# Scores of the second layer issued one span of keys at a time, two small softmax operations folded into others, and the last norm stored by halves

## The chip, the cores and the metric

The kernel runs on one core of a Trainium2 chip. The metric is the device time of one execution in microseconds; an engine is named as the profile names it (PE is TensorE, DVE VectorE, ACT ScalarE, POOL GpSimd, SP SyncE). The change is compared with the kernel before by the median of several runs.

## The reference, cut to what matters

A trunk of two layers over 1024 tokens of width 1024, all in float32. Layer 0 mixes tokens by dilated windows and is not touched. Layer 1 is causal differential attention with 8 heads; each head has two attention maps over the same values, and the second is subtracted from the first.

```python
s = jnp.einsum('bqhcd,bkhcd->bchqk', qblk, k).astype(jnp.float32) * scale   # c: the two maps
s = jnp.where(kpos[None, :] <= qpos[:, None], s, -jnp.inf)
p = jax.nn.softmax(s, axis=-1)
a = p[:, 0] - lam * p[:, 1]
o = jnp.einsum('bhqk,bkhd->bqhd', a, v)
...
o = rmsnorm(o, subln) * (1.0 - lambda_init)
y = o.reshape(B, S, DIFF_WIDTH) * jax.nn.silu(gate)
h = h + rmsnorm(y @ w_out, norm_post[i])
```

## The kernel before

Float32 products are made of two halves: each operand is split into a high and a low part, and a product is three matmuls (`wh` with `XH`, `wh` with `XL`, `wl` with `XH`; the low by the low is dropped). A matmul is 128 x 128 by up to 512 columns. A PSUM tag (`pj` for projections, `s` for scores, `pt` for transposes, `u` for outputs) has two banks that take turns.

TensorE's order is the program's own (`manual_schedule`); the order on the other engines and of the DMAs is set by the compiler's scheduler from its own estimate. On TensorE layer 1 mixes two streams. The first is a list of *steps*, each with a due time in units of heads, sorted by it. The second is a *filler*, a generator of the projections of later heads (`pqk`), values (`pv`), gates (`pg`) and, at the end, the first part of the output product (`pe`). After each step, `fill.at` runs filler until as much of it is spent as belongs to that step's due time:

```python
for _, (due, step) in steps:
    step()
    fill.at(max(due, 0) / end * len(heads))
```

So a step itself stands in the queue right behind the filler of the step before it.

The steps of a head are these. `load(part)` fetches one map's queries (`qh`, `ql`) and keys (`ka`) through SyncE; there are two buffers for each tag, so the load for a head waits until the scores of the same map in the head before have been read. `scores(i, s)` is for block i of 128 queries (0 to 7) and map s: the block has (i + 1) x 128 keys, in one span for blocks 0 to 3 and in two spans for blocks 4 to 7, each of which takes one `s` bank. TensorE writes a span (`sc`, two matmuls); VectorE adds the mask and takes the row's minimum on the way into the tile `pm` (`CUSTOM_DVE_ANT_0`, L954; scores are negated, so the minimum is the largest), with a short read of the accumulated value behind it. With two spans the two minima are joined (L957); for map 0 a constant of 10 ln 2 is taken off (L960), which makes the stored probabilities 2^10 times as large. Then ScalarE takes the exponential of the whole row with its sum (L961). For map 1, VectorE makes the factor (L970, L971) and subtracts the map from map 0 (L973); `pm0` of the block is then final. `pm1` has a single buffer.

`transposes(c, k2)` turns four 128 x 128 squares of the blocks 2c and 2c+1 on TensorE (`tp`, L984), and splits them into `ph` (ScalarE, L989) and `pl` (VectorE, `low` at L122). `product(c, k2)` multiplies them by the values (`ob`, L1004). `norm` and `gate` finish half a head; `gate` ends with two stores of `y_d` through SyncE.

At the end `out_rest` runs the output product for 8 blocks of 128 tokens (`po`, L391), and `post_norm` on each: two sums out of PSUM (`pn`, L492), squares on ScalarE, `pss` and `v` on VectorE, the power -1/2 on GpSimd (`r`), then `pn` times `r` times g (L496) and the sum with the residual `hb` (L497), stored as one DMA of 512 KB.

## Time and profile before

| | |
|---|---|
| median of 3 runs | 1971.28 us (1967.11 to 1976.27) |
| profiled execution | 1973.98 us, its span 1972.1 us |
| TensorE busy | 1888.0 us, 96% of the span |
| VectorE busy | 985.4 us, 50% |
| ScalarE busy | 885.3 us, 45% |
| GpSimd busy | 784.2 us, 40% |
| mean granted TensorE clock | 0.986 |

A row of instructions gives line, engine, operation, what is written and what is read, shape and count; behind the bar the busy time in us and the mean ns of one; behind the next bar the time for which its engine stood idle just before, and what ended it. A row in order of time begins with its start and its length in us and ends, in brackets, with the idle time before it. A row of waits gives who waited for whom: us in total, times, longest. Layer 1's heads run from about 1430 to 1880 us.

### The profile page before, as it was taken

Reading aid. Unit: us, or ns where it says so; the run is one execution under the profiler, and the core shown is the slowest. Engines: PE = TensorE matmul, PEld = TensorE weight load, DVE = VectorE, ACT = ScalarE, POOL = GpSimd, SP = SyncE. Lnnn points to the kernel's source line nnn. Section 1 sums busy time; section 2 is a strip of 40 time slices with the busy share of each in tenths; the row PEclk is TensorE's granted clock in tenths of the full one; section 3 lists DMA queues with packets and bytes.
Section 4 is the critical chain, followed back from the end, with each engine's and each line's share of the span. In section 5 each row is a group of like instructions: output and inputs, shape, how many; then the busy total and the mean of one; then the engine's idle time right before and its main releaser. Section 6 shows DMA issues by size and latency. Waiting matters only on the chain.

```text
span 1972.1 us, 29075 instructions
## 1 busy us (share of the span) xinstructions
PE 1888.0 (96%) x10008; PEld 1587.9 (81%) x10008; DVE 985.4 (50%) x2618; ACT 885.3 (45%) x2043; POOL 784.2 (40%) x553
## 2 busy tenths in 40 slices
PE   7999999999999999999999878999989899999897
PEld 5788888888888888888888767788878798897786
DVE  5311221135555555555555635550177877778626
ACT  4212112135656565656565555342244455446532
POOL 0000001154585867676776532320742435423011
PEclk9999999999999999999999979999999999999899
DMA  6424344277798989898989798442644565556643
GB/s 225 161 91 133 117 145 155 91 233 219 213 294 239 296 242 283 249 280 259 271 267 267 237 329 217 165 167 87 207 155 132 181 213 182 166 182 196 239 158 128
DMA packets 217539, 397.90 MB, mean 202 GB/s; under 512 B 40880, under 2 KB 123312, under 8 KB 217392
## 3 DMA queue, kind: packets, MB, share of 16 engines
q1 hardware_dynamic: 217392, 396.04, 63.8%
q8 instruction: 80, 1.31, 0.3%
q14 instruction: 67, 0.55, 0.1%
HBM read 254.87 MB, written 132.71 MB: 197 GB/s over the span
## 4 chain that ended last, share of the span: by engine, by line
PE 74%; DMA 10%; DVE 7%; POOL 3%; ACT 3%; issue 2%; SPq 1%; POOLq 0%; ACTq 0%; DVEq 0%
PE pqk L276 29%; PE pv L213 17%; PE pg L276 8%; PE po L391 4%; PE sc L603 3%; PE sc L951 3%; PE pe L444 2%; PE tp L626 2%; PE up L653 2%; PE ob L1004 2%; DMA ql<-qk_d 2%; DMA raw<-in_dil_w_out_dram 1%; DMA qk_d<-r 1%; PE tp L984 1%; DMA wb<-wt_d 1%
## 5 line engine op out<-in xcount | busy, mean ns | idle before, releaser
L276 PE MATMUL pqk<-XL,wh 128*128 128x512 f32 x1024 | 418.7, 409 | 0.0
L276 PE MATMUL pqk<-XH,wh 128*128 128x512 f32 x1024 | 408.3, 399 | 1.7 <-DVE t L252 1.7
L276 PE MATMUL pqk<-XH,wl 128*128 128x512 f32 x1024 | 408.6, 399 | 0.0
L122 POOL TENSOR_TENSOR wl<-raw,wh 128x1024 fp32r<-128x1024 f32 x59 | 141.7, 2401 | 512.3 <-ACT wh L184 509.7
L613 ACT ACTIVATE pm<-pm,st 128x128 f32<-128x128 f32 (+1 forms) x384 | 170.4, 444 | 149.5 <-DVE st L610 148.6
L276 PEld LDWEIGHTS pqk<-XH,wh 128*128 128x128 f32 x1024 | 193.2, 189 | 31.5 <-DVE t L252 3.5
L276 PEld LDWEIGHTS pqk<-XH,wl 128*128 128x128 f32 x1024 | 193.5, 189 | 26.9
L276 PEld LDWEIGHTS pqk<-XL,wh 128*128 128x128 f32 x1024 | 193.1, 189 | 26.9
L122 DVE TENSOR_TENSOR pp<-tp,pp 128x512 fp32r<-128x512 f32 (+2 forms) x192 | 104.3, 543 | 132.5 <-ACT pp L630 131.7
L184 ACT CAST wh<-raw 128x1024 fp32r<-128x1024 f32 x96 | 100.6, 1047 | 144.4 <-PE pqk L276 65.8
L961 ACT ACTIVATE pm<-pm,mx 128x256 f32<-128x256 f32 (+7 forms) x128 | 99.4, 777 | 126.8 <-DVE mx L960 61.1
L213 PE MATMUL pv<-vwh,XH 128*128 128x512 f32 x384 | 153.0, 398 | 2.0 <-ACT XH L158 2.0
L213 PE MATMUL pv<-vwh,XL 128*128 128x512 f32 x384 | 153.0, 398 | 2.0 <-DVE XL L122 1.3
L213 PE MATMUL pv<-vwl,XH 128*128 128x512 f32 x384 | 152.2, 396 | 0.0
L122 DVE TENSOR_TENSOR vs<-pv,vs 128x512 fp32r<-128x512 f32 x64 | 44.2, 690 | 202.2 <-ACT vs L518 194.7
L610 DVE CUSTOM_DVE_ANT_0 pm<-sc,masks 128x128 f32<-128x128 f32 (+1 forms) x384 | 119.1, 345 | 27.2 <-PE sc L603 26.5
L630 ACT CAST pp<-tp 128x512 fp32r<-128x512 f32 (+2 forms) x192 | 89.6, 467 | 80.7 <-PE up L653 62.2
L954 DVE CUSTOM_DVE_ANT_0 pm<-sc,md 128x512 f32<-128x512 f32 (+3 forms) x192 | 102.6, 551 | 38.0 <-PE sc L951 35.5
L122 DVE TENSOR_TENSOR wl<-raw,wh 128x1024 fp32r<-128x1024 f32 x37 | 49.1, 1326 | 137.0 <-ACT wh L184 136.7
L251 POOL TENSOR_TENSOR r<-t 128x512 f32<-128x512 f32 x64 | 84.4, 1319 | 80.2 <-DVE t L250 79.1
L518 ACT CAST vs<-pv 128x512 fp32r<-128x512 f32 x48 | 28.1, 586 | 186.8 <-PE pv L213 186.8
L276 PE MATMUL pg<-XH,wh 128*128 128x512 f32 x256 | 103.1, 403 | 5.0 <-DVE t L252 5.0
(514 smaller groups left out, 4435.4 us busy)
## 6 DMA issues: line engine op xcount, KB each, us to landing
qk_d<-rh SPq DMA_DIRECT2D x64, 512.0 KB
qk_d<-r SPq DMA_DIRECT2D x64, 512.0 KB
qh<-qk_d SPq DMA_DIRECT2D x128, 256.0 KB
ql<-qk_d SPq DMA_DIRECT2D x128, 256.0 KB
ka<-qk_d SPq DMA_DIRECT2D x64, 512.0 KB
v_d<-vs SPq DMA_DIRECT2D x48, 512.0 KB
raw<-in_dil_qk_dram SPq DMA_DIRECT2D x48, 512.0 KB
vt<-v_d SPq DMA_DIRECT2D x48, 512.0 KB
```

The source lines that it names most:

```text
L122: return eng.tensor_tensor(o, full, hi.bitcast(F32), ALU.subtract)
L184: nc.scalar.copy(wh, raw)
L213: nc.tensor.matmul(o, lhsT=l, rhs=r_, start=first and k == 0, stop=last and k == 3 * KT - 1, skip_group_check=True)
L251: nc.gpsimd.tensor_sub(put(r[0]), nat(t1), nat(t2))
L276: nc.tensor.matmul(o, lhsT=l[:, kt, :], rhs=r_[:, kt, tok], start=kt == 0 and k == 0, stop=kt == KT - 1 and k == 2)
L391: nc.tensor.matmul(banks[c], lhsT=l[:, kt, ts(n)], rhs=r_[:, ts(c, 512)], start=first and k == 0, stop=last and k == 2,)
L603: nc.tensor.matmul(sc[:, cols], lhsT=q[:, ts(b)], rhs=kv, start=k == 0, stop=k == 1)
L610: nc.vector.tensor_tensor_reduce(pm[:, cols], sc[:, cols], m[:, m.shape[1] - w_ :], 1.0, 3.0e38, ALU.add, ALU.min, st[:, 0, j : j + 1])
L613: nc.scalar.activation(pm[:, cols], pm[:, cols], AF.Exp, bias=st[:, 0, j : j + 1], scale=-1.0, accum_out=st[:, 1, j : j + 1])
L630: nc.scalar.copy(pp[:, 0, :w_], tp[:, :w_])
L954: nc.vector.tensor_tensor_reduce(pm[:, k0:k1], sc[:, :w_], m_, 1.0, 3.0e38, ALU.add, ALU.min, mx[:, j : j + 1])
L961: nc.scalar.activation(pm[:, :wq], pm[:, :wq], AF.Exp, bias=mx[:, 0:1], scale=-1.0, accum_out=den)
```

## The change

Three things. First, `scores` takes one span at a time. A block with two spans has two steps for each map, whose due times are a quarter and three quarters of the way through the map's share, instead of one at its half.

Second, the two small operations go. The second span's reduction starts from the first span's minimum instead of a constant, so that its own result is the minimum of both; and the factor 2^10 is no longer put in by way of the exponent but taken care of where the transposes are split (`ph` and `pl` are scaled by `DEN_SHIFT` = 2^-10), with the constants of the norm adjusted.

Third, in the last norm VectorE multiplies by g without waiting for `r`, and then does each half of the row in one instruction with its own store.

```diff
+            @staticmethod
+            def spans(i):
+                wq = (i + 1) * P
+                cut = wq - max(256, wq - 512) if wq > 512 else 0
+                return [(0, cut), (cut, wq)] if cut else [(0, wq)]
...
-            def scores(self, i, s):
+            def scores(self, i, s, j):
...
-                for j, (k0, k1) in enumerate(spans):
...
-                    nc.vector.tensor_tensor_reduce(
-                        pm[:, k0:k1], sc[:, :w_], m_, 1.0, 3.0e38, ALU.add, ALU.min, mx[:, j : j + 1])
-                if cut:
-                    nc.vector.tensor_tensor(mx[:, 0:1], mx[:, 0:1], mx[:, 1:2], ALU.min)
-                if s == 0:
-                    nc.vector.tensor_scalar_add(mx[:, 0:1], mx[:, 0:1], -10 * math.log(2.0))
+                k0, k1 = self.spans(i)[j]
...
+                nc.vector.tensor_tensor_reduce(
+                    pm[:, k0:k1], sc[:, :w_], m_, 1.0, mx[:, 0:1] if j else 3.0e38,
+                    ALU.add, ALU.min, mx[:, j : j + 1])
+                if k1 < wq:
+                    return
                 nc.scalar.activation(
-                    pm[:, :wq], pm[:, :wq], AF.Exp, bias=mx[:, 0:1], scale=-1.0, accum_out=den)
+                    pm[:, :wq], pm[:, :wq], AF.Exp, bias=mx[:, j : j + 1], scale=-1.0, accum_out=den)
...
-                nc.scalar.copy(ph[:, :w_], tp[:, :w_])
-                low(nc.vector, pl[:, :w_], tp[:, :w_], ph[:, :w_])
+                nc.scalar.mul(ph[:, :w_], tp[:, :w_], DEN_SHIFT)
+                nc.vector.scalar_tensor_tensor(
+                    pl[:, :w_], tp[:, :w_], DEN_SHIFT, ph[:, :w_].bitcast(F32), ALU.mult, ALU.subtract)
...
             for i in range(NB):
+                n = len(hd.spans(i))
                 for s in range(2):
-                    due = h + SPAN * (i * (i + 1) + (s + 0.5) * (i + 1)) / 72
-                    steps.append((due, lambda hd=hd, i=i, s=s: hd.scores(i, s)))
+                    for j in range(n):
+                        due = h + SPAN * (i * (i + 1) + (s + (j + 0.5) / n) * (i + 1)) / 72
+                        steps.append((due, lambda hd=hd, i=i, s=s, j=j: hd.scores(i, s, j)))
...
-        nc.vector.scalar_tensor_tensor(t, t, r, g_b, ALU.mult, ALU.mult)
-        eng.tensor_add(res, t, res)
-        return res
+        if eng is nc.vector:
+            nc.vector.tensor_mul(t, t, g_b)
+            for c in range(2):
+                cols = ts(c, 512)
+                nc.vector.scalar_tensor_tensor(
+                    res[:, cols], t[:, cols], r, res[:, cols], ALU.mult, ALU.add)
+                yield cols, res
...
-            nc.sync.dma_start(out_v[n], o)
+            for cols, o in post_norm(op, n, p0, p1, cos, hb, nc.vector):
+                nc.sync.dma_start(out_v[n][:, cols], o[:, cols])
```

What it makes of the order, at three places. Up to layer 1 the order is the same. The first place is TensorE's queue in head 1 at block 4. `sc` are scores (two matmuls to a span), `pqk` projections of a later head. Before, the two spans of map 0 and, five projections on, those of map 1:

```order
L951 MATMUL sc_14200<-ka_13904,qh_13902 128x384
L951 MATMUL sc_14200<-ka_13904,ql_13903 128x384
L951 MATMUL sc_14204<-ka_13904,qh_13902 128x256
L951 MATMUL sc_14204<-ka_13904,ql_13903 128x256
L276 MATMUL pqk_14161<-XH_78,wh_14147 128x512
L276 MATMUL pqk_14161<-XL_79,wh_14147 128x512
L276 MATMUL pqk_14161<-XH_78,wl_14148 128x512
L276 MATMUL pqk_14161<-XH_78,wh_14147 128x512
L276 MATMUL pqk_14161<-XL_79,wh_14147 128x512
L951 MATMUL sc_14218<-ka_13918,qh_13916 128x384
L951 MATMUL sc_14218<-ka_13918,ql_13917 128x384
```

Now, at the same place:

```order
L967 MATMUL sc_14180<-ka_13888,qh_13886 128x384
L967 MATMUL sc_14180<-ka_13888,ql_13887 128x384
L277 MATMUL pqk_14141<-XH_78,wh_14127 128x512
L277 MATMUL pqk_14141<-XL_79,wh_14127 128x512
L277 MATMUL pqk_14141<-XH_78,wl_14128 128x512
L277 MATMUL pqk_14141<-XH_78,wh_14127 128x512
L967 MATMUL sc_14188<-ka_13888,qh_13886 128x256
L967 MATMUL sc_14188<-ka_13888,ql_13887 128x256
L277 MATMUL pqk_14141<-XL_79,wh_14127 128x512
L277 MATMUL pqk_14141<-XH_78,wl_14128 128x512
L277 MATMUL pqk_14141<-XH_78,wh_14127 128x512
L967 MATMUL sc_14198<-ka_13902,qh_13900 128x384
```

Four of the projections moved between the two spans, and three stand ahead of map 1.

The second place is the end of the same head on TensorE: block 7, map 1. Before, both spans stand together, and behind them come 20 projections, 6 products, 3 transposes and 4 small sums (`sm`) until the first transpose that reads blocks 6 and 7 (`tp_14614`):

```order
L951 MATMUL sc_14494<-ka_13918,qh_13916 128x512
L951 MATMUL sc_14494<-ka_13918,ql_13917 128x512
L951 MATMUL sc_14498<-ka_13918,qh_13916 128x512
L951 MATMUL sc_14498<-ka_13918,ql_13917 128x512
L276 MATMUL pqk_14447<-XH_78,wl_14154 128x512
```

Now ten projections, the 6 products and the 3 transposes stand between the first span (`sc_14463`) and the last (`sc_14492`), and this is all that is left ahead of that transpose:

```order
L967 MATMUL sc_14492<-ka_13902,ql_13901 128x512
L277 MATMUL pqk_14411<-XH_78,wh_14133 128x512
L277 MATMUL pqk_14411<-XL_79,wh_14133 128x512
L277 MATMUL pqk_14411<-XH_78,wl_14134 128x512
L1044 MATMUL sm_14524<-ones_12631,sq_14421 128x1 x4
L277 MATMUL pqk_14574<-XH_78,wh_14560 128x512
L277 MATMUL pqk_14574<-XL_79,wh_14560 128x512
L277 MATMUL pqk_14574<-XH_78,wl_14561 128x512
L277 MATMUL pqk_14574<-XH_78,wh_14560 128x512
L277 MATMUL pqk_14574<-XL_79,wh_14560 128x512
L277 MATMUL pqk_14574<-XH_78,wl_14561 128x512
L999 MATMUL tp_14582<-ident_80,pm0_14297 128x128
```

The transpose kept its place, and the last span moved towards it (one more projection, the tenth, stands right ahead of the transpose and is left out here). On SyncE the loads that follow these scores, for map 1 of head 2, stood so before, with the stores of `y_d` among them:

```order
L268 DMA qh_14548<-qk_d_67 64x1024 x2
L268 DMA ql_14549<-qk_d_67 64x1024
L384 DMA y_d1_64<-sq_14283 128x512
L384 DMA y_d1_64<-os__14282 128x512
L268 DMA ql_14549<-qk_d_67 64x1024
L270 DMA ka_14550<-qk_d_67 128x1024
```

and stand so now, behind the stores and the load of a gate:

```order
L1066 DMA sil_in_14661<-sil_d1_66 128x512
L385 DMA y_d1_64<-sq_14261 128x512
L385 DMA y_d1_64<-os__14260 128x512
L269 DMA qh_14516<-qk_d_67 64x1024 x2
L269 DMA ql_14517<-qk_d_67 64x1024 x2
L271 DMA ka_14518<-qk_d_67 128x1024
```

The third place is VectorE's queue at the very end, the last block's norm. Before:

```order
L492 TENSOR_TENSOR pn_19016<-po_18986,XH_78 128x512
L497 TENSOR_TENSOR hb_18968<-pn_18972,hb_18968 128x1024
L492 TENSOR_TENSOR pn_19016<-po_18987,XL_79 128x512
L494 TENSOR_TENSOR pss_19015<-s2_19014 128x1
L134 TENSOR_SCALAR v_19023<-pss_19015 128x1
L496 SCALAR_TENSOR_TENSOR pn_19016<-pn_19016,r_19024,cos_2235 128x1024
L497 TENSOR_TENSOR hb_19012<-pn_19016,hb_19012 128x1024
```

and now (`cos` holds g here):

```order
L493 TENSOR_TENSOR pn_18902<-po_18872,XH_78 128x512
L502 SCALAR_TENSOR_TENSOR hb_18852<-pn_18856,r_18864,hb_18852 128x512 x2
L493 TENSOR_TENSOR pn_18902<-po_18873,XL_79 128x512
L495 TENSOR_TENSOR pss_18901<-s2_18900 128x1
L499 TENSOR_TENSOR pn_18902<-pn_18902,cos_2235 128x1024
L135 TENSOR_SCALAR v_18909<-pss_18901 128x1
L502 SCALAR_TENSOR_TENSOR hb_18898<-pn_18902,r_18910,hb_18898 128x512 x2
```

The product with g stands between `pss` and `v`, and the pairs of halves take the places of the two instructions of the full row.

## The prediction

> **What bounds the kernel now.** I read the page first, then one window over the stage that the change touches (layer 1's heads, from the first score to the last transposes), then TensorE's waits, and last the order of time around single waits.

> ```profile
> span 1972.1 us, 29075 instructions
> PE 1888.0 (96%) x10008; PEld 1587.9 (81%) x10008; DVE 985.4 (50%) x2618; ACT 885.3 (45%) x2043; POOL 784.2 (40%) x553
> PE 74%; DMA 10%; DVE 7%; POOL 3%; ACT 3%; issue 2%; SPq 1%; POOLq 0%; ACTq 0%; DVEq 0%
> 1430.00:1880.00 450.00, 418.44 (x2571) 367.89 (x2569) 341.33 (x937) 235.98 (x464) 164.11 (x112) 0.98 0.57 183
> ```

> TensorE is the bound, and its instructions are the same before and after. Its queue runs in program order, so the change can only move the time by what TensorE waits, by its clock, and by what lies behind its last matmul. The last row is the stage (columns as on the page: PE, PEld, DVE, ACT, POOL busy, clock, DMA share): 450 us, TensorE idle for 31.6, VectorE busy for 341.3, 76%, the fullest engine beside it. TensorE's waits of the whole run:

> ```profile
> PE sc L951 <- DVE mx L954: 17.9, 16, 2.5
> PE sc L951 <- DMA ka<-qk_d: 7.8, 2, 6.7
> PE pv L213 <- DVE vs L122: 2.9, 1, 2.9
> PE tp L984 <- DVE pm L973: 2.6, 4, 0.9
> ```

> All four lie in this stage. The first is what the change is about: a score needs one of two PSUM banks, and VectorE has not yet reduced what stands in it. By the width of the span that waits (idle time behind the bar):

> ```profile
> L951 PE MATMUL sc<-ka,qh 128*128 128x512 f32 x80 | 34.4, 430 | 6.2 <-DVE mx L954 6.1
> L951 PE MATMUL sc<-ka,qh 128*128 128x384 f32 x48 | 17.8, 370 | 4.2 <-DVE mx L954 4.2
> L951 PE MATMUL sc<-ka,qh 128*128 128x256 f32 x48 | 15.3, 318 | 7.8 <-DVE mx L954 7.6
> ```

> It is no steady lack of VectorE time (76%), but a queue that is late at moments. One of them, block 4 of head 0:

> ```profile
> 1441.20 1.61 DVE L973 SCALAR_TENSOR_TENSOR pm<-pm,mx,pm 128x384 f32<-128x384 f32 x1
> 1442.73 1.22 DVE L1030 TENSOR_TENSOR nd<-den 128x4 f32<-128x4 f32 x1
> 1443.88 0.68 DVE L954 CUSTOM_DVE_ANT_0 pm<-sc,md 128x512 f32<-128x512 f32 x1
> 1444.62 0.39 PE L951 MATMUL sc<-ka,qh 128*128 128x256 f32 x1 [1.75 <-DVE mx L954]
> ```

> **Part 1, the small operations.** The rows that price them (busy, mean ns):

> ```profile
> L957 DVE TENSOR_TENSOR mx<-mx 128x1 f32<-128x1 f32 x64 | 22.8, 357 | 0.7
> L960 DVE TENSOR_SCALAR mx<-mx 128x1 f32<-128x1 f32 x64 | 9.5, 148 | 0.7
> L122 DVE TENSOR_TENSOR pl<-tp,ph 128x512 fp32r<-128x512 f32 x45 | 30.8, 684 | 1.7 <-ACT ph L989 1.6
> L1047 DVE SCALAR_TENSOR_TENSOR os__15635<-os__15635,subln,rt 128x512 f32<-128x512 f32 x1 | 0.7, 748 | 0.0
> L957 DVE TENSOR_TENSOR mx<-mx x64: 147/154/2250, 1446.0 to 1877.7; 128x1 f32<-128x1 f32 x64
> ```

> The minimum of two spans (L957) and the shift by a factor of 2^-10 (L960) go: 22.8 + 9.5 = 32.3 us of VectorE. The low half `pl` turns from a two-operand into a scaled three-operand instruction; the nearest row that reads PSUM, a tile and a scalar (L1047) takes 748 against 684, so 80 of them add at most 80 x 0.064 = 5.1. The second span's reduction now starts from a column instead of a constant; no row shows that form, and I bound it by nothing and by the same 0.064 each, 64 x 0.064 = 4.1, and take 2. The scaled copy `ph` on ScalarE (236 of 450 us busy) is hidden by the slack of that engine; without it, it would lengthen the step from a transposition to its product, which the program sets 0.2 of a head apart, some 11 us of 56. So VectorE gives up 32.3 - 5.1 - 2 = 25 us, 7% of its 341. None of this is on the path by itself; it makes the queue late less often. L957 has a minimum of 147 ns and a longest of 2250: it is held up at times, where L960 (mean 148) is not.

> **Part 2, the spans apart.** Where a block has two spans, their scores stood back to back and now have filler between. The order shows that a bank's turn (from one score in it to the next but one) keeps its length on the whole: in head 1 at block 4 the second span of the first map moves away by four projections, but the first span of block 6's first map moves closer to what it waits for. What improves is that two reductions no longer arrive at once. Bounds: all 17.9 us go, or 4 come on top (at two of the sixteen places in a head turns shrink by about 1.3 and 2.4 us, to 1.8; a quarter of those missed by 1 us is 4). The waits in single-span blocks (part of the 256 and 384 rows) keep their turn and gain only from part 1. I take half, -9.0.

> One wait of the kind, of 2.53 us at 1462, is followed by a slower clock (column before DMA share):

> ```profile
> 1460.00:1464.00 4.00, 1.46 (x7) 1.03 (x8) 4.00 (x10) 1.75 (x2) 2.72 (x2) 1.00 0.34 134
> 1464.00:1467.50 3.50, 3.50 (x20) 3.50 (x19) 2.85 (x6) 1.89 (x3) 0.00 (x0) 0.51 0.39 152
> ```

> TensorE was busy for 1.46 of 4 us, and then 3.5 us ran at 0.51: 1.7 us lost. The bank of that score gets about 1 us more turn; I count the loss as gone, -1.7 (ends -1.7 and 0). [...]

> **Part 3, the price of moving the last span.** A step runs as soon as the step before it has had its filler. So the last span of a block no longer stands at the previous step's due time but at its own first half's, nearly a whole step later, while the transposes that need the block keep their due times. Head 1, block 7, second map, before:

> ```profile
> 1531.10 0.40 PE L951 MATMUL sc<-ka,ql 128*128 128x512 f32 x1
> 1534.02 0.68 DVE L954 CUSTOM_DVE_ANT_0 pm<-sc,md 128x512 f32<-128x512 f32 x1
> 1535.24 0.08 DVE L954 DVE_READ_ACCUMULATOR2_ANT mx<- 128x1 f32 x1
> 1536.09 1.15 ACT L961 ACTIVATE pm<-pm,mx 128x1024 f32<-128x1024 f32 x1 [1.35 <-DVE mx L957]
> 1538.20 1.27 DVE L973 SCALAR_TENSOR_TENSOR pm<-pm,mx,pm 128x1024 f32<-128x1024 f32 x1
> 1538.35 0.33 PE L984 MATMUL tp<-ident,pm 128*128 128x128 f32 x1 [0.26 <-DVE pl L122]
> 1539.54 0.55 PE L984 MATMUL tp<-ident,pm 128*128 128x128 f32 x3 [0.86 <-DVE pm L973]
> ```

> From the score's end (1531.3) to the first transpose TensorE had 6.8 us of other work, and it still waited 0.86. In the new order ten projections (0.23 each), six products (0.12) and three transposes (0.12) of that work stand ahead of the last span: 3.3 us less, 3.4 left. Counted so in the order, the heads keep about 3.4 (0 and 1), 4.7 (2 to 5) and 3.6 (6 and 7). The chain needs at least 0.1 + 0.69 (reduction and its read) + 0.1 + 3.38 (1536.09 to 1539.47) = 4.3 us; measured it took 8.1, of which 2.7 passed before the first reduction and 1.2 with the first reduction and L957, which no longer stand there: 7.0 at most. Per head the wait is then between nothing and 3.5. Floor: (4.3 - 3.4) x 2 + (4.3 - 3.6) x 2 = 3.2; ceiling: 8 x 7.0 - (2 x 3.4 + 4 x 4.7 + 2 x 3.6) = 23. VectorE is 7% emptier there, so I take a value nearer the floor, 1.2 per head, 9.6; 2.6 of it is there already: +7.0 (ends +0.6 and +21). In head 1 ScalarE's queue also holds a weight's high half and a projection's copy ahead of the exponential.

> The same delay reaches SyncE: the next head's second load reuses the buffers that the last span reads.

> ```profile
> 1475.41 1.09 SPq L268 DMA_DIRECT2D qh<-qk_d  x2
> 1477.83 0.58 SPq L270 DMA_DIRECT2D ka<-qk_d  x1
> 1532.47 0.55 SPq L268 DMA_DIRECT2D ql<-qk_d  x1
> 1536.83 0.58 SPq L270 DMA_DIRECT2D ka<-qk_d  x1
> 1824.68 0.72 SPq L270 DMA_DIRECT2D ka<-qk_d  x1
> 1833.42 0.47 PE L951 MATMUL sc<-ka,qh 128*128 128x128 f32 x1 [6.75 <-DMA ka<-qk_d]
> ```

> `ka` is issued 2.4 us after the last score at the earliest and lands up to 8.7 us later (1824.68 to 1833.42). Its cover shrinks by the same 3.3 us, but in heads where a store of `y_d` stood among the loads (4.4 us from `ql` to `ka` at 1532) the new order has the stores ahead of `qh`. I take no change: 7.8 stays (ends -5, if the stores were what made head 7 late, and +14, two more us in each of seven heads).

> **Part 4, the last norm.**

> ```profile
> 1963.29 0.68 DVE L492 TENSOR_TENSOR pn<-po,XL 128x512 f32<-128x512 f32 x1
> 1964.76 0.16 DVE L494 TENSOR_TENSOR pss<-s 128x1 f32<-128x1 f32 x1 [0.79 <-ACT pq L493]
> 1965.83 1.28 DVE L496 SCALAR_TENSOR_TENSOR pn<-pn,r,cos 128x1024 f32<-128x1024 f32 x1 [0.72 <-POOL r L135]
> 1967.15 1.23 DVE L497 TENSOR_TENSOR hb<-pn,hb 128x1024 f32<-128x1024 f32 x1
> 1968.40 0.33 SPq L1104 DMA_DIRECT2D out_dram<-hb  x1
> ```

> The product with g no longer needs `r`, but VectorE's order puts it behind `pss` and ahead of `v`, the start of the way to `r`, and not into the 0.79 us ahead of `pss`. So 1.22 us (as L497) enters the chain to `r`, and 1.28 + 1.23 turn into two halves of about 0.70: the last half is ready about 0.2 us later than before. Its store carries half the bytes; of the 3.7 us from 1968.40 to the span's end that takes between nothing and half, 1.8, and since it has a fixed part that I can't see I take 0.6. Together -0.4 (ends -1.6 and +0.2). The other seven blocks' norms lie beside TensorE's `po`; eight more stores cost SyncE 0.33 each, with nothing waiting behind them.

> **The sum** against the profiled execution, 1974.0 us: -9.0 - 1.7 + 7.0 + 0 - 0.4 = -4.1, so 1969.9. That execution lies 2.7 above the median of the runs, 1971.3; on the median it makes 1967.2.

> **Rivals.**
> - *The queue clears.* 25 us less of VectorE and reductions that come singly end nearly all waits for banks, and the transposes wait no longer than before: -17.9 - 1.7 - 0.4, so 1951.3. For it: VectorE at 76% has slack, the waits are few (16). Against it: 3.4 us of cover against a chain of at least 4.3.
> - *The transposes take it back and more*, the one that ends slower. Its place is the first transpose of blocks 6 and 7 in every head. At the ceiling it is +21 instead of +7: 1981.2. If each wait then also brings the 1.7 us of slow clock that followed 2.53 us, 8 x 1.7 more: 1994.8. It decides from a wait of about 3 us per head on. [...]
> - *The loads come late* in the next head as well: +10 at 1.4 us in seven heads, so 1977; against it, every us that the transposes wait is cover for the load.
> - *The change doesn't do what it says*: banks are late for what stands in VectorE's queue (1441 to 1444 above), not for pairs of reductions; the waits go elsewhere, and the time stays at 1971.

> **How the numbers follow.** My forecast 0.45, the queue clears 0.20, transposes 0.14, loads 0.07, nothing 0.14. About 0.5% (9.9 us) is what a measurement of this kernel can tell from no change. Faster by more needs 1961.4: most of the second case and the lower edge of mine (1958 to 1979 is its own range), 0.24. Slower by more needs 1981.1: the third case and a little of the others, 0.17. Within: 0.59. The range leaves out a tenth on each side: 1953 to 1984.

> **What would show it.** TensorE's wait for `mx` at the scores at 9 instead of 17.9; its wait for `pm` at the transposes near 10 instead of 2.6, with the longest in heads 0 and 1; VectorE's busy time in the stage down by about 25; the product with g between `pss` and `v`, and the last store shorter but no earlier. I am wrong if the transposes wait no longer than now, if waits for `ka` appear in each head, or if the waits for `mx` stay at 18.

## The result, and the profile after

The changed kernel takes 2002.4 us (median of 6 runs, 1997.8 to 2006.7) against 1971.9 for the kernel before on the same chip: a ratio of 1.0155 with a 95% interval of 1.0132 to 1.0177. The forecast was 1967.2, with a range that ended at 1984. The profiled execution took 1997.8 us. From the head of its page:

```profile
span 1996.0 us, 29032 instructions
PE 1895.5 (95%) x10008; PEld 1596.0 (80%) x10008; DVE 975.9 (49%) x2498; ACT 888.8 (45%) x2043; POOL 783.8 (39%) x553
```

The span grew by 23.9 us. TensorE's 10008 instructions are the same, but take 7.5 us more (1895.5 - 1888.0), and TensorE stands idle for 16.4 us more (100.5 against 84.1). So in this pair of executions two thirds of the loss are waits, and one third is slower work. (The medians lie 30.5 us apart; the executions that were profiled, 1997.8 and 1974.0, lie 23.8 apart, and the account below is of these two.) The waits for layer 1's steps, TensorE's view (us in total, times, longest):

```profile
PE sc L967 <- DMA ka<-qk_d: 31.2, 7, 8.0
PE tp L999 <- DVE pm L988: 10.5, 5, 6.0
...
PE sc L967 <- DVE mx L971: 6.8, 9, 1.5
...
PE tp L999 <- DMA ka<-qk_d: 1.0, 1, 1.0
PE tp L999 <- DVE os__17444 L1064: 0.6, 1, 0.6
PE tp L999 <- DVE nd L1050: 0.4, 1, 0.4
```

Scores wait for their bank (`mx`) 6.8 us instead of 17.9, transposes for VectorE 11.5 (`pm`, `os` and `nd` together). Both are near the forecast, 9 and 9.6. What is new is the first row: the next head's scores wait for `ka` 31.2 us instead of 7.8. By the width of the span that waits, all of it stands at the first block of a head:

```profile
L967 PE MATMUL sc<-ka,qh 128*128 128x128 f32 x16 | 5.4, 336 | 31.2 <-DMA ka<-qk_d 31.2
```

Head 3's second map, SyncE's DMA issues and TensorE in order of time. TensorE's last read of the old buffers, block 7's last `sc` with `ql`, starts at 1596.66 (the last row is the same place a head later):

```profile
1596.66 0.39 PE L967 MATMUL sc<-ka,ql 128*128 128x512 f32 x1
...
1598.06 0.38 SPq L1066 DMA_DIRECT2D sil_in<-sil_d  x1
1598.54 0.57 SPq L262 DMA_DIRECT2D qk_d<-r  x1
1599.20 0.54 SPq L385 DMA_DIRECT2D y_d<-sq  x1
1599.83 0.44 SPq L385 DMA_DIRECT2D y_d<-os__14873  x1
1600.36 0.49 SPq L269 DMA_DIRECT2D qh<-qk_d  x1
1600.95 1.86 SPq L868 DMA_DIRECT2D v_d<-vs  x2
1603.27 0.52 SPq L269 DMA_DIRECT2D qh<-qk_d  x1
1604.03 1.70 SPq L269 DMA_DIRECT2D ql<-qk_d  x2
1605.97 0.39 SPq L271 DMA_DIRECT2D ka<-qk_d  x1
...
1613.48 0.47 PE L967 MATMUL sc<-ka,qh 128*128 128x128 f32 x1 [7.02 <-DMA ka<-qk_d]
...
1671.48 0.33 PE L967 MATMUL sc<-ka,qh 128*128 128x128 f32 x1 [1.90 <-DMA ka<-qk_d]
```

The buffers are free at about 1597, but SyncE first issues four other DMAs, until `qh` goes at 1600.36. Two stores of `v_d` stand among the loads, `ka` is issued 9 us late, and TensorE can use it 7.5 us after that. The stretches around it, and around the shorter wait of 1.90 us at 1671.48 (columns as in the prediction: busy time of PE, PEld, DVE, ACT, POOL, then granted clock, DMA share, GB/s):

```profile
1600.36:1613.48 13.12, 5.07 (x42) 4.63 (x40) 4.10 (x12) 2.39 (x6) 1.02 (x1) 0.89 1.03 326
1606.00:1610.50 4.50, 0.46 (x4) 0.25 (x3) 0.67 (x1) 0.00 (x0) 0.00 (x0) 1.00 1.06 295
1610.50:1617.30 6.80, 3.82 (x18) 3.83 (x19) 1.03 (x5) 0.49 (x2) 0.00 (x0) 0.50 0.55 166
...
1664.50:1671.90 7.40, 5.37 (x30) 4.10 (x29) 2.72 (x6) 2.51 (x5) 2.85 (x4) 1.00 1.00 319
1671.90:1675.40 3.50, 3.50 (x16) 3.23 (x15) 3.24 (x6) 1.01 (x3) 3.23 (x2) 0.51 0.13 13
```

Two things are to be read here. From the first `qh` to the use of `ka` the DMA engines are full (1.03): they move 4.27 MB in these 13.1 us, and the load itself is 1 MB of that. I read this so that `ka` lands when the engines get to it; whether its slot in SyncE's queue matters as well is tested below. And the clock is halved: 6.8 us at 0.50 at the long wait, of which the first 3.0 are its end and 3.8 are work, and 3.5 us at 0.51 behind the short one. That is the slower work on the page: in layer 1's heads the trace has seven such stretches, 47.8 us together, where the kernel before has three, 17.1 us.

### The profile page after: what moved, and what is told of

Same layout as the page of the kernel before. It is cut to its first block, busy times and chain, and to the rows that moved or that the text cites. A ratio compares the mean times of both kernels' runs of the same rounds, so it can differ in the third digit from the quotient of the medians.

```text
span 1996.0 us, 29032 instructions
## 1 busy us (share of the span) xinstructions
PE 1895.5 (95%) x10008; PEld 1596.0 (80%) x10008; DVE 975.9 (49%) x2498; ACT 888.8 (45%) x2043; POOL 783.8 (39%) x553
## 4 chain that ended last, share of the span: by engine, by line
PE 80%; DMA 8%; DVE 5%; ACT 2%; issue 2%; POOL 1%; SPq 1%; DVEq 0%; POOLq 0%; ACTq 0%
PE pqk L277 32%; PE pv L214 16%; PE pg L277 8%; PE sc L613 4%; PE po L392 4%; PE pe L445 3%; PE tp L636 3%; PE up L663 3%; PE sc L967 3%; DMA ka<-qk_d 2%; PE ob L1021 2%; DMA raw<-in_dil_w_out_dram 1%; PE tp L999 1%; DVE pm L971 1%; DMA ql<-qk_d 1%
## 5 line engine op out<-in xcount | busy, mean ns | idle before, releaser
L277 PEld LDWEIGHTS pqk<-XH,wl 128*128 128x128 f32 x1024 | 194.2, 190 | 26.5
L620 DVE CUSTOM_DVE_ANT_0 pm<-sc,masks 128x128 f32<-128x128 f32 (+1 forms) x384 | 119.1, 346 | 27.4 <-PE sc L613 26.5
L967 PE MATMUL sc<-ka,qh 128*128 128x512 f32 (+2 forms) x192 | 73.5, 383 | 38.2 <-DMA ka<-qk_d 31.2
```

What stands on the lines that cost most here:

```text
L277: nc.tensor.matmul(o, lhsT=l[:, kt, :], rhs=r_[:, kt, tok], start=kt == 0 and k == 0, stop=kt == KT - 1 and k == 2)
L620: nc.vector.tensor_tensor_reduce(pm[:, cols], sc[:, cols], m[:, m.shape[1] - w_ :], 1.0, 3.0e38, ALU.add, ALU.min, st[:, 0, j : j + 1])
L967: nc.tensor.matmul(sc[:, :w_], lhsT=q[:, ts(i)], rhs=ka[:, k0:k1], start=k == 0, stop=k == 1)
```

## The experiments

T-load is the theory that block 7's last scores now come too late for the next head's loads. The main rival, T-transposes, says that the longer chain from scores to transposes is the cause, and that the loads only follow. All runs were timed beside the kernel before, and a ratio is against that on the same chip. *loads* are waits of scores and transposes of layer 1 for a DMA, *tp* those of transposes and of the norm's sums for an engine, *mx* those of scores for their bank, all in us of the profiled execution. A wait without a releaser in the trace is in none of them; such waits at scores are 3.6 us in x6, 5.0 in x8 and 3.6 in x13.

| run | median us | ratio to before (95%) | loads | tp | mx |
|---|---|---|---|---|---|
| before | 1971.9 | | 7.8 | 3.3 | 17.9 |
| after | 2002.4 | 1.0155 (1.0132 to 1.0177) | 32.2 | 11.5 | 6.8 |
| x1_norm | 1974.8 | 1.0000 (0.9984 to 1.0016) | 7.2 | 2.8 | 18.4 |
| x2_small | 1973.9 | 0.9992 (0.9978 to 1.0006) | 6.9 | 2.6 | 17.2 |
| x3_spans | 1999.1 | 1.0115 (1.0089 to 1.0141) | 26.5 | 17.8 | 9.8 |
| x4_lastpair | 1966.1 | 0.9969 (0.9954 to 0.9984) | 9.8 | 3.8 | 13.1 |
| x5_late | 1998.3 | 1.0122 (1.0094 to 1.0150) | 17.9 | 17.5 | 14.4 |
| x6_lag | 1976.5 | 1.0011 (0.9996 to 1.0026) | 9.3 | 4.4 | 15.5 |
| x7_kafirst | 2005.9 | 1.0163 (1.0138 to 1.0187) | 34.3 | 12.5 | 7.3 |
| x8_kasplit | 2011.8 | 1.0192 (1.0161 to 1.0222) | 32.6 | 12.5 | 7.9 |
| x9_after_noload | 1954.1 | 0.9895 (0.9877 to 0.9913) | 0 | 11.9 | 8.0 |
| x10_before_noload | 1956.1 | 0.9905 (0.9888 to 0.9923) | 0 | 2.9 | 17.7 |
| x11_last1 | 1982.1 | 1.0050 (1.0027 to 1.0073) | 22.3 | 0.9 | 11.8 |
| x12_earlier | 1962.3 | 0.9936 (0.9917 to 0.9954) | 6.1 | 3.2 | 12.8 |
| x13_last0 | 1986.8 | 1.0066 (1.0049 to 1.0084) | 15.6 | 12.0 | 9.3 |
| x14_early_pairs | 1976.3 | 1.0024 (1.0009 to 1.0040) | 11.1 | 3.8 | 14.6 |
| x15_earlier_q | 1967.7 | 0.9974 (0.9958 to 0.9991) | 9.1 | 1.0 | 14.0 |

**Which part of the change.** x1 is the kernel before with the change to `post_norm` alone, x2 with `DEN_SHIFT` and the chained minimum alone, x3 with the steps by spans alone.

> The kernel before with the last norm alone changed (g multiplied ahead, result in halves). If the last norm has a part in the lost time, this run is slower than before by more than 0.2%. By the prediction's term it is 0.4 us faster: the time from the end of the last po matmul to the end of the span falls from 10.55 us to about 10.1, and all waits of TensorE stay as before (sc on mx about 18 us, sc on ka about 8 us). I expect the second.

> The kernel before with the small operations alone folded (chained minimum, the factor 2**-10 in the copies of P), scores still in pairs. The prediction's theory: VectorE loses some 30 us of busy time, the waits of sc on mx (17.9 us) fall by 2 to 8 us because the chained minimum saves one small operation in front of the exponentials, the ka waits stay at 8 us, the time is 1966 to 1972 us. Rival: the scaled copy and the low half with a scalar cost more in place than their rows say, or the lighter VectorE brings the last scores forward and the loads late; then the time is 1980 us or more and the ka waits exceed 15 us.

> The kernel before with the steps by spans alone; the minimum and shift operations stay. Theory T-load (the last span of block 7's second map comes half a step later, so that the next head's second ka is asked for later and TensorE waits for it, and each such wait is followed by a stretch of half clock): ka waits of sc 25 to 35 us in six or seven places, transposes on pm 8 to 14 us, sc on mx 6 to 10 us, time 1998 to 2008 us. Rival (the folding of the small operations is at fault, the spans are not): ka waits about 8 us, sc on mx halved, 1960 to 1968 us.

By themselves the norm and the small operations change nothing that can be measured; the spans alone lose 1.15% by the same waits, with 17.8 us at the transposes where 8 to 14 were expected. x1's last 11.2 us (from the start of the last block's first `pn`) are no shorter than before (10.55), so its forecast of 10.1 failed. The changed kernel, with the same norm, has 10.1 there; from the last norm instruction's end to the span's end it is 4.3 us in x1 and 3.2 in the changed kernel, more of a difference than the change was to make. Before it was 3.7 us with twice the bytes in the last store, so in neither run does this time follow the bytes. In x2 the banks' waits fell by 0.7 us, not by 2 to 8.

**Block 7's pairs put back.** x4 is the changed kernel with:

```diff
+                    if i == NB - 1:
+                        due = h + SPAN * (i * (i + 1) + (s + 0.5) * (i + 1)) / 72
+                        steps.append((due, lambda hd=hd, i=i, s=s, n=n: [hd.scores(i, s, j) for j in range(n)]))
+                        continue
```

> The changed kernel with one edit: block 7's two spans of each map are one step again, due where the pair was due before, so that the next head's loads are asked for as early as before; blocks 4 to 6 stay in spans. T-load: the ka waits fall from 31 us to about 8 us, most stretches of half clock go, transposes on pm fall to 3 to 6 us because block 7 was where they waited, sc on mx rises from 7 us to 8 to 11 us; 1960 to 1972 us. Rival T-transposes (the longer chain from the last span to the transposes of all four blocks is the cause, and the loads come late only because everything ahead of them does): ka waits stay above 15 us, 1985 us or more.

```profile
PE sc L967 <- DVE mx L971: 13.1, 16, 2.2
PE sc L967 <- DMA ka<-qk_d: 9.8, 3, 6.5
PE tp L999 <- DVE pm L988: 1.4, 2, 1.2
```

The time and the waits for loads and transposes are those of T-load (the banks' 13.1 us are more than its 8 to 11), and the run is 0.3% faster than before. So it is block 7's spans that turn a small gain into a loss. But the edit puts the loads and the transposes back together.

**Only the place, no spans.** x5 is the kernel before with one number changed:

```diff
-                    due = h + SPAN * (i * (i + 1) + (s + 0.5) * (i + 1)) / 72
+                    due = h + SPAN * (i * (i + 1) + (s + (0.75 if s and i == NB - 1 else 0.5)) * (i + 1)) / 72
```

> The kernel before with one number changed: in block 7 the pair of score spans of the second map is due a quarter of a step later (s + 0.75 for s + 0.5). No span step, no folded operation. In TensorE's order this puts the pair behind the projection group that it stood ahead of, so that between block 7's last scores and the next head's first scores of the second map stand 8708 to 9220 columns of matmul (6660 for the last head) where 15748 to 17796 (12164) stood, the same as in the changed kernel. T-load (the place of the last scores of the second map alone makes the loss): ka waits 24 to 34 us in six or seven places, 1992 to 2006 us. Rival (the loss needs the span steps themselves: their switches between score, projection and transposes): ka waits 8 to 12 us, 1969 to 1978 us.

```profile
PE sc L951 <- DMA ka<-qk_d: 15.1, 4, 10.6
PE sc L951 <- DVE mx L954: 14.4, 12, 2.5
PE tp L984 <- DVE pm L973: 13.7, 6, 5.2
PE tp L984 <- DMA ql<-qk_d: 2.8, 1, 2.8
```

The time came as T-load said, so the place of the pair alone costs 1.2%. The split didn't: 17.9 us for loads, less than the 24 to 34 expected, and 17.5 at the transposes. Against the kernel before, this is 14.2 us more at the transposes and 10.1 more for loads. The transposes stand ahead of the next head's scores in the queue, and while TensorE waits there, a load has time to land. Time and waits alone don't part the theories.

**Later transposes.** x6 is the changed kernel with `LAG` 0.38 for 0.3.

> The changed kernel with LAG 0.38 for 0.3: transposes and what follows from them come later against the scores, all span steps stay. The last scores of the second map now stand 18052 to 18308 columns of matmul ahead of the next head's first ones (13700 at the last head), more than before the change. T-load: ka waits 2 to 8 us, transposes on pm 0 to 3 us, sc on mx about 7 us as in the changed kernel, 1955 to 1965 us. Rival T-transposes (the cause is the longer chain of score, exponential and transposes, which drags the loads behind it): the longer chain is then merely moved behind, waits appear at what follows (ob, sm, the y stores, the loads that these stores hold up), 1975 us or more.

Neither picture came. The time is the rival's, but load waits of 9.3 us, 3.6 more at a score without a releaser in the trace, and banks' waits back at 15.5 are neither's. What holds this run up stays open.

**The load itself.** Both start from the changed kernel. x7 issues layer 1's `ka` ahead of `qh` and `ql`; x8 leaves its place and loads it as two DMAs:

```diff
-            nc.sync.dma_start(ka.bitcast(F32), qk_d[unit, 1, h].rearrange("l e f t -> (l e f) t"))
+            for l in range(2):
+                nc.sync.dma_start(
+                    ka[64 * l : 64 * l + 64].bitcast(F32), qk_d[unit, 1, h, l].rearrange("e f t -> (e f) t"))
```

> The changed kernel with layer 1's ka load issued ahead of the four loads of qh and ql rather than behind them; order of all steps untouched. If the issue queue in front of ka sets the lateness (ka issued 2.9 to 9 us after the last score, of which 1.3 to 6 lie between qh and ka), the six waits of 31 us in all fall to 12 to 20 us (now on ql, which comes last) and the time to 1980 to 1990 us. If the 1 MB of the five transfers together sets it (whichever comes last lands no earlier), the waits of sc on ka and ql together stay at 26 to 33 us, and the time at 1998 to 2004 us. Under T-transposes nothing changes: 2002 us.

> The changed kernel with layer 1's ka load as two transfers of 64 partitions (256 KB each, like those of qh and ql) where one of 128 partitions stood. If the single transfer of 512 KB is slow by its form (its packets took 280 ns in the changed kernel, those of qh and ql 159 ns), ka lands about 2 us earlier in each of six heads: ka waits 31 us to about 18 us, 1986 to 1993 us. If the transfers share one bandwidth, or the time lies in the queue ahead of ka, nothing changes but one more issue of 0.6 us per load: ka waits 29 to 35 us, 2000 to 2006 us.

x7's waits (first two rows):

```profile
PE sc L970 <- DMA qh<-qk_d: 20.0, 5, 7.4
PE sc L970 <- DMA ql<-qk_d: 14.3, 8, 3.7
```

The wait moves to whatever comes last, 34.3 us in all, and x8 gains nothing either; both end above the time expected of them (2005.9 against at most 2004, 2011.8 against at most 2006). Neither the order of the five transfers nor the form of `ka`'s sets the lateness. What is left is their 1 MB together, on DMA engines that are full with this and other traffic: in the changed kernel a share of 1.03 over head 3's load, at 326 GB/s, reads and writes together, and of 1.02 over head 5's (1720.85 to 1735.86), at 373 GB/s.

**The second map's loads left out**, from the changed kernel and from the one before:

```diff
-                self.fin.append(heads_in(ep, 24 + self.h, part))
+                self.fin.append(heads_in(ep, 24 + self.h, part) if part == 0 else self.fin[0])
```

> The changed kernel with layer 1's second map reading the first map's q and k: the second map's own five loads per head are left out, and with two buffers for one set of tiles per head no load of q and k has to wait for the last scores. The order of all TensorE's instructions is that of the changed kernel. It leaves out half of layer 1's loads of q and k, so it is read against the next run, which leaves out the same. T-load: no waits on ka, transposes on pm still 8 to 15 us, most stretches of half clock gone, 1950 to 1964 us, and level with or below the next run. Rival T-transposes: the loads only follow; the time stays 1985 us or more, and 15 us or more above the next run.

> The kernel before with the same loads left out, as the base for the run ahead. Its ka waits of about 8 us and the half clock behind them go: 1956 to 1968 us under both theories.

TensorE's waits in x9, then in x10:

```profile
PE tp L999 <- DVE pm L988: 11.3, 6, 6.0
PE sc L967 <- DVE mx L971: 8.0, 12, 1.2
```

```profile
PE sc L951 <- DVE mx L954: 17.7, 17, 2.5
PE tp L984 <- DVE pm L973: 2.1, 3, 0.9
```

This parts the theories. The transposes wait as long as in the changed kernel (11.9 us), and still x9 is 2.0 us below x10, their intervals overlapping. Without these loads the change is about neutral: 9.0 us more at the transposes against 9.7 less at the banks. With them it costs 30.5 us. So the loads, with the slow clock that comes with them, are worth some 32 us, and T-transposes is out as the cause of the loss, though the longer chain does cost its 9 us.

**Which map.** x11 keeps block 7's second map alone in a pair (`if i == NB - 1 and s:` in x4's edit), x13 the first (`and not s`).

> The changed kernel with the two spans of block 7's second map alone in one step, due where the pair was due before; all other maps and blocks stay in spans. Between its last scores and the next head's first ones stand 15748 to 17284 columns of matmul, as before the change. T-load: ka waits about 8 to 10 us, sc on mx 8 to 11 us (13 with both maps of block 7 paired), 1960 to 1968 us. Rival (both maps' last spans matter): ka waits above 15 us, 1980 us or more.

> The mirror of the run that paired block 7's second map alone: the changed kernel with the two spans of block 7's first map in one step, due where the pair was due before, and the second map in spans, its last scores 8708 to 9220 columns ahead of the next head's first ones as in the changed kernel. If the second map's own cover alone decides, 1990 to 2004 us. If both decide (too little cover for the second map's load, and the first map's load in front of it on the same transfers), the waits on ka lie between: 12 to 22 us, and the time 1976 to 1990 us. If only the first map's place decides, 1960 to 1970 us.

x11 was to be as fast as x4, and lost 0.5%: the second map's cover does not decide alone. x13 lies between, as the theory of both maps has it. From x11's SyncE and TensorE, into head 6:

```profile
1772.48 1.13 SPq L269 DMA_DIRECT2D qh<-qk_d  x2
...
1774.94 0.58 SPq L271 DMA_DIRECT2D ka<-qk_d  x1
1775.62 1.08 SPq L269 DMA_DIRECT2D qh<-qk_d  x2
...
1779.49 0.33 SPq L271 DMA_DIRECT2D ka<-qk_d  x1
...
1787.83 0.33 PE L967 MATMUL sc<-ka,qh 128*128 128x128 f32 x1 [1.89 <-DMA ka<-qk_d]
```

The first map's load is asked for only 3.1 us ahead of the second's. In x4 these two lie 6.0 us apart:

```profile
1753.55 1.14 SPq L269 DMA_DIRECT2D qh<-qk_d  x2
...
1759.53 1.08 SPq L269 DMA_DIRECT2D qh<-qk_d  x2
```

In x11 all of TensorE's waits for loads but 0.9 us stand at the second map's first scores, although that map's last scores have their old place. With the DMAs nearly full (a share of 0.97 from 1772.48 to 1787.83), the second map's megabyte comes on top of the first's. Counted from x4 (0.9969), the first map late costs 0.0081 (x11), the second 0.0097 (x13), and both 0.0186 (the changed kernel): within intervals of about 0.002 to each side, the two add up.

**All in spans, but earlier.** x12 and x15 take `(n - 1) * 0.5` or `(n - 1) * 0.25` from the due time of each two-span step:

```diff
-                        due = h + SPAN * (i * (i + 1) + (s + (j + 0.5) / n) * (i + 1)) / 72
+                        due = h + SPAN * (i * (i + 1) + (s + (j + 0.5) / n - (n - 1) * 0.5) * (i + 1)) / 72
```

> The changed kernel with the due times of all two-span steps half a step earlier (the last span where the pair stood, the first ahead of it); everything stays in spans. Between the last scores of the second map and the next head's first ones stand 15748 to 17284 columns, as before the change. T-load: ka waits about 8 to 10 us, transposes on pm 1 to 4 us, sc on mx 7 to 10 us, 1955 to 1966 us. Rival T-transposes (the span steps themselves lengthen the chain): 1980 us or more.

> The changed kernel with all two-span steps a quarter step earlier rather than half a step: the last span is due exactly where the pair was due before, the first half a step ahead of it; 15236 to 15748 columns between the second map's last scores and the next head's first ones (before 15748 to 17796). T-load: ka waits 8 to 14 us, 1958 to 1970 us. If the first map's last scores matter as much as the second's, the same, since both have their old place. Rival (a quarter step is not enough, the waits come back): 1975 us or more.

TensorE's waits in x12:

```profile
PE sc L967 <- DVE mx L971: 12.8, 13, 2.0
...
PE sc L967 <- DMA ka<-qk_d: 6.1, 3, 2.7
...
PE tp L999 <- DVE os__17450 L1064: 2.2, 1, 2.2
```

Both beat both kernels: x12 by 0.64% over the kernel before, x15 by 0.26%, little, but with intervals that end below 1. In x12 the last span is due at s + 0.25, a quarter step ahead of the pair before; "where the pair stood" in its expectation is true of TensorE's order, not of the due time. The banks' waits were to be 7 to 10 us and are 12.8, so not all of the gain at the banks survives the earlier place.

x14 is the kernel before with its pairs earlier (0.25 for 0.5 in blocks 4 to 7):

> The kernel before with one number changed: pairs of blocks 4 to 7 are due a quarter step earlier (s + 0.25 for s + 0.5), no span steps, no folding; in TensorE's order the last scores keep the columns ahead of the next head's first ones that they had before (15748 to 17796). If the gain of the fastest run (all steps by spans, half a step earlier) is only the earlier place, this run gains it too: 1958 to 1966 us. If it is the spans (fewer waits of sc on mx) with the place kept, this run stays at 1968 to 1976 us, with sc on mx 15 to 19 us.

It is 0.24% slower, not faster. So an earlier place alone is no gain; the changed kernel in that place is. That the gain lies in the banks is not shown: x14 waits for them 14.6 us, hardly more than x15 (14.0), and less than was expected of it. x15 waits less at the transposes (1.0 against 3.8) and for loads (9.1 against 11.1). It differs from x14 by the spans and by the folded operations, and no run parts these two in the early place.

A third buffer for `qh`, `ql` and `ka` would let the loads start ahead of the last scores. No run tries it.

## Why the prediction was wrong

- **The step that failed** is in part 3, the loads: "I take no change: 7.8 stays (ends -5 ... and +14 ...)". It measured +24.4 us of waits (7.8 to 32.2), beyond the upper end, and the slow clock on top (below). The prediction had the mechanism (the next head's load reuses the buffers that the last span reads), saw `ka` land 8.7 us after its issue, and then let two guesses cancel the lost cover. The first was that the stores of `y_d` would now go ahead of `qh` and so do no harm. They do go ahead, but in head 3 `qh` is issued 3.3 us after the buffers are free, behind a gate's load, another store and these two, which take 1.1 us of SyncE's time. The second was "every us that the transposes wait is cover for the load". That is so (x5, and head 2 after the change, where the transposes waited and `ka` did not), but the transposes wait for more than 2 us in two heads alone (1 and 7).
- It also followed only one map's load. Both maps' loads share full DMA engines (a share of 0.97 from 1772.48 to 1787.83 in x11), and the first map's span moved too; x11 and x13 give each about half.
- **The slow clock** was counted as a gain of 1.7 us and as a price in one rival only, for the transposes. In layer 1 of the changed kernel a slow stretch at 0.50 goes with each of the six waits of 3.9 us or more (3.90 to 7.99): 7.5 us more of TensorE work. The prediction held a row that says so (2.53 us of wait, then 0.51), and the 1.90 us wait above says it again. But such a wait is not enough each time. This one, the last of the changed kernel's heads, is followed by more than 6 us at 1.00:

```profile
1905.78 0.55 PE L999 MATMUL tp<-ident,pm 128*128 128x128 f32 x3 [2.25 <-DVE pm L988]
```

- **Together**, between the two profiled executions: -11.1 for banks, +8.2 at transposes, +24.4 for loads and +7.5 by the clock make +29.0; the span grew by 23.9. The other 5 us are smaller waits elsewhere that fell, such as the 2.9 us of `pv` for `vs` in the prediction's rows.
- **The spans** were right in kind and size: -9.0 forecast for the banks, -11.1 measured (-9.7 from x10 to x9, 17.7 to 8.0).
- **The transposes** were right: +7.0 forecast, +8.2 measured (3.3 to 11.5). The longest is in head 1, as said (6.0 us; head 0, named with it, waits 0.6). VectorE's queue there:

```profile
1536.13 0.74 DVE L971 CUSTOM_DVE_ANT_0 pm<-sc,md,mx 128x512 f32<-128x512 f32 x1
...
1537.40 1.22 DVE L123 TENSOR_TENSOR wl<-raw,wh 128x1024 fp32r<-128x1024 f32 x1
...
1539.52 1.22 DVE L1052 TENSOR_TENSOR nr<-nr,nd 128x4 f32<-128x4 f32 x1 [0.90 <-POOL nr L1051]
...
1540.84 1.23 DVE L986 SCALAR_TENSOR_TENSOR mx<-mx,neg_lam,den 128x1 f32<-128x1 f32 x1
1542.11 2.26 DVE L988 SCALAR_TENSOR_TENSOR pm<-pm,mx,pm 128x1024 f32<-128x1024 f32 x1
...
1544.42 0.90 PE L999 MATMUL tp<-ident,pm 128*128 128x128 f32 x3 [6.04 <-DVE pm L988]
```

  A weight's low half and a norm's factor stand between the reduction and the subtraction, and that takes 2.26 us here against 1.27 in the row of before. The 3.4 us of cover that were left are not enough for this.
- **The small operations** were right in being worth little by themselves (x2), but VectorE's busy time fell by less than the 25 us of the forecast: by 15.4 in x2 (970.0 against 985.4), and in layer 1's heads by 10.6 in the changed kernel (341.3 to 330.7). Of the terms, the low half `pl` costs nothing more (686 ns against 684, where 748 was feared). A reduction that starts from a column takes 746 ns against 684, so 64 of them some 4 us and not 2:

```profile
L971 DVE CUSTOM_DVE_ANT_0 pm<-sc,md,mx 128x512 f32<-128x512 f32 x16 | 11.9, 746 | 4.3 <-PE sc L967 4.1
```

  The two rows of 32.3 us went. But part of their time was no time of VectorE's own: in the trace a small operation lies beside its neighbours, as here in the kernel before, where L957 starts with the read ahead of it and ends behind the start of the next instruction:

```profile
1463.75 0.08 DVE L954 DVE_READ_ACCUMULATOR2_ANT mx<- 128x1 f32 x1
1463.75 0.15 DVE L957 TENSOR_TENSOR mx<-mx 128x1 f32<-128x1 f32 x1
1463.82 1.22 DVE L122 TENSOR_TENSOR r<-r,rh 128x1024 fp32r<-128x1024 f32 x1
```

  The rows of all VectorE's instructions add up to 25 us less in x2, the forecast's figure, though by other terms than its own, which is luck; in the busy time, where such overlaps count once, 15.4 are left.
- **The last norm** can't be told from nothing (forecast -0.4; x1 at 1.0000 with an interval of 0.0016 to each side).
- Of the rivals, "the loads come late" was the right one. It had 0.07 and +10 us; it measured +24.4 in waits, and its share of the clock on top.

## What to carry to other kernels

When a step is moved later, follow what its last read sets free, for every queue, and not only the chain that it feeds: here the buffers' next loads lost more than the banks gained, and a shift of the due times by half a step, with the spans kept, turned 1.6% slower into 0.6% faster. With the DMA engines full, as here (a share of 0.97 to 1.03 over these loads), ask how early a load is asked for and what else is asked for at the time: its order and form gained nothing here (34.3 and 32.6 us of waits against 32.2). Where the clock falls with waits, as it did here, price each new long wait with the slow stretch that comes with it (3.4 to 10.2 us at 0.50).
